# Sending the q and k norms and the softmax's inverse sums through DRAM in a two-layer hybrid block

## The chip, the cores and the metric

One core of a Trainium2 chip runs the whole program. Its engines are PE (TensorE, matrix products into PSUM), DVE (VectorE), ACT (ScalarE), POOL (GpSimd) and SP (SyncE, which here only issues transfers). Each executes its own list of instructions in order and waits on semaphores of the others. The metric is device microseconds of one execution, median of several runs; lower is better.

## The reference

Two layers over 256 latent tokens with a prefix of 256 context tokens, model width 1024. A layer normalizes and modulates its input, projects it, and feeds three branches: a state-space scan ("ssd"), attention, and a gated MLP. Their outputs are projected, gated and summed; then comes a SwiGLU. The part that matters here is attention:

```python
def rmsnorm(t, w):
    tf = t.astype(jnp.float32)
    tf = tf * lax.rsqrt(jnp.mean(tf * tf, axis=-1, keepdims=True) + EPS)
    return tf.astype(t.dtype) * w
...
    return rmsnorm(q, q_norm), rmsnorm(k, k_norm), v      # 8 heads of 64 features
...
    p = softmax(concatenate([s_lat, s_ctx]))               # latent queries: 512 keys, with a bias
    out = p @ [v_lat, v_ctx]
    s = q @ k.T * Dh ** -0.5; p = softmax(s); out = p @ v  # context queries: 256 keys (layer 0 only)
```

So every head's q and k (per token) is multiplied by one over the root of its mean square, and every row of the softmax by one over its sum.

## The kernel before

Activations lie feature by token: 128 features on the partitions, 512 tokens (256 context, 256 latent) along the free axis. Weights come from DRAM in 316 tiles of 128 x 1024 (`wr`, five buffers in the pool `raw`). ACT rounds each to float32r (`hi`, L222), DVE takes the rest (`lo`, L232), and three products of float32r parts stand for one product in float32 (`mm3`, L246). `ws.low` of a tile also has SP load the tile three further on. Tiles `T` (128 x 512) come from a ring of 61, `S` from eight PSUM banks; a tile that is asked for again makes its first writer wait for the last user of the old one.

The order of work is written out by hand. `gemm` (L275) issues the big products and calls `tick` after every fourth k-step. A tick stands for four k-steps of 512 columns (twelve products); it advances the clock, runs what `later` set down for that time, and takes steps of three queues of generators, "ssd", "att" and "mod", at rates of their own (att: 1.0 steps a tick at first, then `R_ATT`, 0.85 in layer 0 and 1.0 in layer 1). Each `yield` ends a step. So small work of the branches is threaded between big products, on all engines at once.

What the change touches:

- `qk_tile` leaves q and k and their squares in SBUF. `qk_norm` (L1066), once for k and once for q in each layer, sums the squares of each head by a small product into PSUM (two rows per group of 32 partitions hold the two heads of tile j), takes root and reciprocal of all 128 x 512 values, splits the result into two float32r parts placed on different partitions (`RQ`, L1086 and L1087), and after a few more steps has PE spread it for each j over 128 partitions (`pair_rows`, L1092); DVE multiplies q or k by that (L1094). In layer 1 q has 256 columns.
- `attention` takes head after head. An item is one head of the context or the latent queries: 16 items in layer 0 (ctx, ctx, lat, lat for each pair of heads), 8 in layer 1 (lat only). At step t it issues the output product of the pair that ended at t - 4 (`pv_out`), the transposes of item t - 2 (`transp`), and the scores of item t. Scores: PE, DVE adds the bias and takes the maximum (L1141, L1160), ACT takes the exponential with its row sum. Half a tick later `rest` takes one over the sum and multiplies the probabilities by it (L1148 to L1150, L1169 to L1172), before PE transposes them (L1186).
- `pv_out`: ACT rounds the result from PSUM (L1202), DVE takes the rest from PSUM (L1203).
- `bias_load`: SP refills a ring of four bias tiles at once when their next head is known.

Of the kernel before, what the change touches and what calls it, by code (L numbers as in the profile page):

```python
# [80 lines left out]
D_0 = (3, 6)  # L81
D_1 = (6, 3)
Q_0 = (1, 2)
Q_1 = (3, 5)
Q_2 = (6, 3)
L_G = (4, 4)
Z_S = (1.5, 3.0)
Y_S = (2.0, 0.5)
# [1 line left out]
G_S = (1.0, 0.5)  # L90
F_LAG = (3, 3)
FA = 2


@with_exitstack
def kernel(ctx: ExitStack, tc: tile.TileContext, a, out):
# [19 lines left out]
    def T(s="t", dt=F32):  # L116
        return tpool.tile([128, TOK], dt, tag="t", name=nm(s))
# [25 lines left out]
    for e, f in ((epsb, 1.0), (eps4, 4.0), (eps64, 64.0)):  # L143
        DVE.memset(e, f * EPS)
    mk = cpool.tile([128, 256], F32, name="mk")
    selp = cpool.tile([128, 8, 128], F32R, name="selp")
    lom = cpool.tile([128, 1], F32, name="lom")
    ident = cst[:, C_ID:C_ID + 128]
    ones = cst[:, C_ONE:C_ONE + 128]

# [454 lines left out]
    for l in range(NL):  # L605
# [5 lines left out]
        def pcol(c, n=1):  # L611
            return P[:, c:c + n]
# [32 lines left out]
        if not last:  # L645
            SP.dma_start(out=cst[:, 0:C_ONE], in_=a["cst"][:, 0:C_ONE])
            SP.dma_start(out=cst[:, C_COS:C_ROW], in_=a["cst"][:, C_COS:C_ROW])
            SP.dma_start(out=cst[:, C_BS:C_MF], in_=a["cst"][:, C_BS:C_MF])
            SP.dma_start(out=mk, in_=a["cst"][:, C_MF:NC_])
            DVE.tensor_copy(selp.rearrange("p a (b c) -> p a b c", c=64),  # L650
                            cst[:, C_SP:C_SP + 16].rearrange("p (a b) -> p a b", b=2).unsqueeze(3).to_broadcast(
                                [128, 8, 2, 64]))

            DVE.tensor_reduce(out=lom, in_=cst[:, C_ROW + 4:C_ROW + 8], op=ADD, axis=AX.X)
            DVE.tensor_scalar(lom, lom, -1.0, None, MUL)

        def token_major(n0, evac, between=()):

# [113 lines left out]

        Fd = dpool.tile([64, 2, 128], F32, name=nm("Fd"))
        Cd = dpool.tile([16, 4, 128], F32, name=nm("Cd"))

        def pair_rows(j, pr):

            return selp[:, 2 * j + pr]

        def dt_gen():  # L780
            for _ in range(D_0[l]):
# [284 lines left out]
        def qk_norm(kind):  # L1066

            b = 0 if kind == "k" else c0
            for _ in range(Q_0[l]):
                yield  # L1070
            ps = S()
            for j in range(4):
                mm(ps[32 * j:32 * j + 32, b:], cst[:, C_BS:C_BS + 32], qsq.pop((kind, j))[:, b:])
            rq, RQ = T("rq"), T("RQ", F32R)
            if kind == "q":
                ACT.activation(rq[:, b:], ps[:, b:], AF.Sqrt, bias=eps64)
            else:
                ACT.activation(rq[:, b:], ps[:, b:], AF.Sqrt, scale=1.0 / 64, bias=epsb)
            table(AF.Exp)
            for c in range(b, 512, 256):  # L1080
                DVE.reciprocal(rq[:, c:c + 256], rq[:, c:c + 256])
                yield
            for _ in range(Q_1[l]):
                yield

            ACT.copy(RQ[:, b:], rq[:, b:])  # L1086
            DVE.scalar_tensor_tensor(RQ[:, b:], RQ[:, b:].bitcast(F32), lom, rq[:, b:], MUL, ADD)  # L1087
            for _ in range(Q_2[l]):
                yield
            for j in range(4):  # L1090
                ps = S()
                mm(ps[:, b:], pair_rows(j, 0), RQ[:, b:])  # L1092
                t = qk[kind, j]
                DVE.scalar_tensor_tensor(t[:, b:], t[:, b:], pcol(P_KN if kind == "k" else P_QN),  # L1094
                                         ps[:, b:], MUL, MUL)
                yield

        def attention():
# [30 lines left out]
            def score(ps, hd, q0, n):  # L1129
                Q, lo, K = st[hd]  # L1130
                mm(ps, Q[:, q0:q0 + 128], K[:, 0:n], True, False)
                mm(ps, lo[:, q0:q0 + 128], K[:, 0:n], False, True)

            def scores_lat(hd):
                pr = []
                st_ = small(8, "ast")
                for qt in (0, 1):
                    bt = T("bt")
                    ps = S()
                    score(ps, hd, 256 + qt * 128, 512)  # L1140
                    DVE.tensor_tensor_reduce(out=bt, in0=ps, in1=biases[2 * hd + qt], op0=ADD, op1=MAX, scale=1.0,  # L1141
                                             scalar=-3.0e38, accum_out=st_[:, qt:qt + 1])
                    DVE.tensor_scalar(st_[:, 2 + qt:3 + qt], st_[:, qt:qt + 1], -1.0, None, MUL)
                    ACT.activation(bt, bt, AF.Exp, bias=st_[:, 2 + qt:3 + qt], accum_out=st_[:, 4 + qt:5 + qt])
                    pr.append(bt)

                def rest():
                    DVE.reciprocal(st_[:, 6:8], st_[:, 4:6])  # L1148
                    for qt in (0, 1):
                        DVE.tensor_scalar(pr[qt], pr[qt], st_[:, 6 + qt:7 + qt], None, MUL)  # L1150

                later(A_N[l], rest)
                return pr

            def scores_ctx(hd):
                st_ = small(8, "ast")
                ps = S()
                for qt in (0, 1):
                    score(ps[:, qt * 256:qt * 256 + 256], hd, qt * 128, 256)
                DVE.tensor_reduce(out=st_[:, 0:2], in_=ps.rearrange("p (q k) -> p q k", q=2), op=MAX, axis=AX.X)  # L1160
                DVE.tensor_scalar(st_[:, 2:4], st_[:, 0:2], -1.0, None, MUL)
                p = T("pc")
                for qt in (0, 1):
                    sl = slice(qt * 256, qt * 256 + 256)
                    ACT.activation(p[:, sl], ps[:, sl], AF.Exp, bias=st_[:, 2 + qt:3 + qt],
                                   accum_out=st_[:, 4 + qt:5 + qt])

                def rest():
                    DVE.reciprocal(st_[:, 6:8], st_[:, 4:6])  # L1169
                    for qt in (0, 1):  # L1170
                        sl = slice(qt * 256, qt * 256 + 256)
                        DVE.tensor_scalar(p[:, sl], p[:, sl], st_[:, 6 + qt:7 + qt], None, MUL)  # L1172

                later(A_N[l], rest)
                return p

            def transp(s_, pr):
# [14 lines left out]
            def pv_out(s_, j, pts):  # L1192
                ps = S()
                nk = 4 if s_ else 2
                for kt in range(nk):
                    for q in (0, 1):
                        hd = 2 * j + q
                        mm(ps[64 * q:64 * q + 64, 0:256], va[kt][:, hd * 64:hd * 64 + 64],
                           pts[q][kt // 2][:, (kt % 2) * 256:(kt % 2) * 256 + 256], kt == 0, kt == nk - 1)
                hi, lo, b = yna[j]  # L1200
                sl = slice(s_ * 256 - b, s_ * 256 + 256 - b)
                ACT.copy(hi[:, sl], ps[:, 0:256])  # L1202
                DVE.tensor_tensor(lo[:, sl], ps[:, 0:256], hi[:, sl], SUB)  # L1203

            items = [(j, s_, q) for j in range(4) for s_ in ((1,) if last else (0, 1)) for q in (0, 1)]
            pr, pts = {}, {}
# [5 lines left out]
            for t in range(len(items) + A_P[l]):  # L1212
# [13 lines left out]
                if t < len(items):  # L1226
                    j, s_, q = items[t]
                    pr[t] = (scores_lat if s_ else scores_ctx)(2 * j + q)
                    if s_ and 2 * j + q < 6:
                        bias_load(2 * j + q + 2)  # L1230
                if heads and (last or t % 2):
                    stack(heads.pop(0))
                yield
# [455 lines left out]
```

## Time and profile before

| | us |
|---|---|
| median of 3 runs (1603.38 to 1606.58) | 1603.64 |
| profiled execution, its own time | 1604.21 |
| its span in the profile | 1602.4 |
| PE, DVE, ACT busy in the span | 1578.7, 1163.1, 830.5 |

The profiled execution's time is 1.8 us longer than its span. PE's granted clock is 0.997 of full speed over the span. "Busy" of PE counts the modelled length of overlapping products: back-to-back products overlap, so the distance from one start to the next says what a product costs, not its length. Layer 0's qk_norms lie at about 140 to 260 us and its attention at about 350 to 460; layer 1's at about 1100 to 1210 and 1235 to 1317.

### The profile page before, as it was taken

To read this page: it belongs to the slowest core of one execution; us is meant where nothing else is said; L and a number is where in the kernel's file an instruction comes from. 1 tells how busy PE (TensorE), PEld (TensorE's weight loads), DVE (VectorE), ACT (ScalarE), POOL (GpSimd) and SP (SyncE) were. 2 spreads that over 40 slices of the span, in tenths; PEclk is the share of its full clock that TensorE was granted. 3 is DMA by queue.
4 is the path that set the end of the run, shared out by engine and by line. 5 is a ranking of instruction groups with operands and counts; after the bars stand their busy time and mean duration, and the time that the engine had idled before them with its cause. 6 is when DMAs were issued, how large, how long until landed. Compare 5 with 4: busy or idle time off the path is not lost.

```text
span 1602.4 us, 23608 instructions
## 1 busy us (share of the span) xinstructions
PE 1578.7 (99%) x8908; PEld 1325.2 (83%) x8909; DVE 1163.1 (73%) x2005; ACT 830.5 (52%) x1551; POOL 6.9 (0%) x21
## 2 busy tenths in 40 slices
PE   8999999999999999999999999999999999999999
PEld 5878787777678888988888888978888989998888
DVE  5467889777868766676666654778988987687764
ACT  4456876656643233433223212667676785466652
POOL 0000000000000000000000000000000000000000
PEclk9999999999999999999999999999999999999999
DMA  9513433443344545354556775525434456656654
GB/s 331 206 53 115 125 105 107 122 141 92 107 135 142 183 148 193 122 177 155 180 172 198 260 241 185 174 92 161 130 115 138 134 157 183 199 167 192 194 178 138
DMA packets 87345, 254.37 MB, mean 159 GB/s; under 512 B 10560, under 2 KB 19008, under 8 KB 87104
## 3 DMA queue, kind: packets, MB, share of 16 engines
q1 hardware_dynamic: 87232, 252.87, 49.3%
q8 instruction: 70, 1.15, 0.3%
q14 instruction: 43, 0.35, 0.1%
HBM read 248.44 MB, written 4.39 MB: 158 GB/s over the span
## 4 chain that ended last, share of the span: by engine, by line
PE 79%; DVE 11%; ACT 5%; DMA 3%; issue 2%; SPq 0%; ACTq 0%; DVEq 0%
PE g L126 71%; PE s L126 6%; DVE lo L232 3%; DVE xbc L718 2%; DMA wm<-in_wmod 2%; ACT hi L222 1%; PE s L1186 1%; ACT M L987 1%; DVE scr L192 1%; DVE bt L1141 1%; DVE M L896 0%; DMA x<-in_xT 0%; ACT rb L987 0%; DVE ks L1114 0%; PE rs L126 0%
## 5 line engine op out<-in xcount | busy, mean ns | idle before, releaser
L126 PE MATMUL g<-hh,hi 128*128 128x512 f32 (+1 forms) x1280 | 471.4, 368 | 0.1
L126 PE MATMUL g<-hh,lo 128*128 128x512 f32 (+1 forms) x1280 | 462.1, 361 | 1.4 <-DVE lo L232 1.4
L126 PE MATMUL g<-hl,hi 128*128 128x512 f32 (+1 forms) x1280 | 462.1, 361 | 0.5 <-DVE hl L551 0.4
L232 DVE TENSOR_TENSOR lo<-wr,hi 128x1024 fp32r<-128x1024 f32 x316 | 382.5, 1219 | 78.1 <-ACT hi L222 77.6
L222 ACT CAST hi<-wr 128x1024 fp32r<-128x1024 f32 x316 | 323.8, 1046 | 37.7 <-DMA wr<-in_ws 31.8
L126 PEld LDWEIGHTS g<-hh,hi 128*128 128x128 f32 x1280 | 241.8, 189 | 49.0 <-issue 11.5
L126 PEld LDWEIGHTS g<-hh,lo 128*128 128x128 f32 x1280 | 241.6, 189 | 40.8 <-DVE lo L232 3.4
L126 PEld LDWEIGHTS g<-hl,hi 128*128 128x128 f32 x1280 | 242.0, 189 | 37.1 <-DVE hl L551 1.1
L192 DVE SCALAR_TENSOR_TENSOR scr<-wm,csil 128x1024 bf16<-128x1024 f32 x128 | 156.1, 1220 | 63.4 <-DMA wm<-in_wmod 63.3
L126 PE MATMUL g<-hp,hi 128*128 128x512 f32 x304 | 105.7, 391 | 0.0
L718 DVE SCALAR_TENSOR_TENSOR xbc<-g,pv,xbc 128x508 f32<-128x508 f32 (+3 forms) x128 | 91.3, 713 | 9.5 <-ACT xbc L712 6.4
L126 PE MATMUL g<-hp,lo 128*128 128x256 f32 x304 | 85.3, 281 | 0.9 <-DVE lo L232 0.8
L1295 ACT ACTIVATE th<-g,pv 128x512 f32<-128x512 f32 (+1 forms) x48 | 27.9, 580 | 95.9 <-PE g L126 91.6
L367 ACT CAST fh<-f 128x512 fp32r<-128x512 f32 x22 | 13.6, 620 | 112.9 <-DVE f L1447 112.9
L126 PE MATMUL g<-fh,lo 128*128 128x512 f32 x176 | 68.6, 390 | 0.4 <-DVE lo L232 0.4
L126 PE MATMUL g<-fh,hi 128*128 128x512 f32 x176 | 68.5, 389 | 0.0
L126 PE MATMUL g<-fl,hi 128*128 128x512 f32 x176 | 68.5, 389 | 0.0
L126 PEld LDWEIGHTS g<-hp,hi 128*128 128x128 f32 x304 | 56.9, 187 | 12.4
L126 PE MATMUL g<-lo,hh 128*128 128x256 f32 x224 | 63.7, 284 | 3.2 <-DVE lo L232 3.1
L126 PE MATMUL g<-hi,hh 128*128 128x256 f32 x224 | 64.6, 288 | 0.0
L126 PE MATMUL g<-hi,hl 128*128 128x256 f32 x224 | 63.3, 283 | 0.0
L126 PE MATMUL g<-fp,hi 128*128 128x512 f32 (+1 forms) x198 | 61.4, 367 | 0.0
(310 smaller groups left out, 2657.9 us busy)
## 6 DMA issues: line engine op xcount, KB each, us to landing
wr<-in_ws SPq DMA_DIRECT2D x316, 512.0 KB, 4.2
wm<-in_wmod SPq DMA_DIRECT2D x80, 512.0 KB, 4.4
rb<-Fd SPq DMA_DIRECT2D x48, 256.0 KB, 3.9
wm<-in_wm SPq DMA_DIRECT2D x32, 256.0 KB, 6.0
ex<-Cd SPq DMA_DIRECT2D x32, 128.0 KB, 3.6
bias<-in_rpb SPq DMA_DIRECT2D x32, 128.0 KB, 2.1
x<-in_xT SPq DMA_DIRECT2D x8, 256.0 KB, 6.1
xm<-in_xT SPq DMA_DIRECT2D x8, 256.0 KB, 5.3
```

The source lines that it names most:

```text
L126: PE.matmul(o, l, r, start=start, stop=stop)
L192: DVE.scalar_tensor_tensor(scr, raws[n], 1.0, csil[:, v, :], MUL, MUL, accum_out=modr[l][:, ft, v:v + 1])
L222: ACT.copy(hi, self.raw[i])
L232: DVE.tensor_tensor(lo, self.raw.pop(i), hi, SUB)
L367: ACT.copy(hi, src[:, c0:])
L718: DVE.scalar_tensor_tensor(av3[:, :, o0:o1], pv3[:, :, o0 + d:o1 + d], w(j), av3[:, :, o0:o1], MUL, ADD)
L987: ACT.activation(z, z, AF.Exp, bias=bias(st, d))
L1141: DVE.tensor_tensor_reduce(out=bt, in0=ps, in1=biases[2 * hd + qt], op0=ADD, op1=MAX, scale=1.0, scalar=-3.0e38, accum_out=st_[:, qt:qt + 1])
L1186: PE.transpose(ps[:, kt * 256 + qt * 128:kt * 256 + qt * 128 + 128], src, ident)
L1295: ACT.activation(th[:, c0:], ps[:, c0:], AF.Tanh, scale=0.5, bias=pcol(P_BG + br * 8 + m))
```

## The change

The spread over partitions by PE and the scaling of the probabilities by DVE are both replaced by transfers through DRAM. The diff, cut to its core:

```diff
-Q_1 = (3, 5)
-Q_2 = (6, 3)
+B_L = (1.0, 0.5)
+I_A = (1.0, 0.75)
+I_B = (1.0, 1.0)
...
-    selp = cpool.tile([128, 8, 128], F32R, name="selp")
-    lom = cpool.tile([128, 1], F32, name="lom")
...
 qk_norm:
-            rq, RQ = T("rq"), T("RQ", F32R)
+            n = 512 - b
+            t, w = T("rq"), small(32, "rqs", 2)
+            Nd, Ni = (dpool.tile([8, n], F32, name=nm("Nd")) for _ in range(2))
+            ACT.copy(t[:, b:], ps[:, b:])
+            yield
+            yield
+            for j in range(4):
+                SP.dma_start(out=Nd[2 * j:2 * j + 2], in_=t[32 * j:32 * j + 2, b:])
+            flat = lambda z: z.rearrange("h t -> (h t)").rearrange("(p c) -> p c", p=128)
+            w = w[:, 0:n // 16]
+            for _ in range(2):
+                yield
+            SP.dma_start(out=w, in_=flat(Nd))
+            for _ in range(2):
+                yield
             if kind == "q":
-                ACT.activation(rq[:, b:], ps[:, b:], AF.Sqrt, bias=eps64)
+                ACT.activation(w, w, AF.Sqrt, bias=eps64)
...
             table(AF.Exp)
-            for c in range(b, 512, 256):
-                DVE.reciprocal(rq[:, c:c + 256], rq[:, c:c + 256])
-                yield
-            for _ in range(Q_1[l]):
-                yield
-            ACT.copy(RQ[:, b:], rq[:, b:])
-            DVE.scalar_tensor_tensor(RQ[:, b:], RQ[:, b:].bitcast(F32), lom, rq[:, b:], MUL, ADD)
-            for _ in range(Q_2[l]):
-                yield
+            DVE.reciprocal(w, w)
+            yield
+            yield
+            SP.dma_start(out=flat(Ni), in_=w)
+            R = {}
+            def spread(j):
+                R[j] = T("RQ")
+                for a_ in (0, 1):
+                    SP.dma_start(out=R[j][64 * a_:64 * a_ + 64, b:],
+                                 in_=Ni[2 * j + a_].unsqueeze(0).to_broadcast([64, n]))
+            yield
+            yield
+            spread(0)
+            yield
+            yield
             for j in range(4):
-                ps = S()
-                mm(ps[:, b:], pair_rows(j, 0), RQ[:, b:])
                 t = qk[kind, j]
+                if j < 3:
+                    spread(j + 1)
                 DVE.scalar_tensor_tensor(t[:, b:], t[:, b:], pcol(P_KN if kind == "k" else P_QN),
-                                         ps[:, b:], MUL, MUL)
+                                         R.pop(j)[:, b:], MUL, MUL)
                 yield
 attention:
+            Pd = dpool.tile([16, 256], F32, name=nm("Pd"))
+            inv = {}
+            def inverse(s_, hd, st_):
+                DVE.reciprocal(st_[:, 6:8], st_[:, 4:6])
+                j, q = divmod(hd, 2)
+                if q == 0:
+                    inv[s_, j] = small(256, "inv", 3)
+                row, y = Pd[s_ * 8 + hd], inv[s_, j]
+                def back():
+                    SP.dma_start(out=y[64 * q:64 * q + 64, :], in_=row.unsqueeze(0).to_broadcast([64, 256]))
+                def away():
+                    SP.dma_start(out=row.rearrange("(q p) -> p q", p=128), in_=st_[:, 6:8])
+                    later(I_B[l], back)
+                later(I_A[l], away)
...
-                    DVE.reciprocal(st_[:, 6:8], st_[:, 4:6])
-                    for qt in (0, 1):
-                        DVE.tensor_scalar(pr[qt], pr[qt], st_[:, 6 + qt:7 + qt], None, MUL)
-                later(A_N[l], rest)
+                later(A_N[l], lambda: inverse(1, hd, st_))
...                                    (the same for the context items)
 pv_out:
-                ACT.copy(hi[:, sl], ps[:, 0:256])
-                DVE.tensor_tensor(lo[:, sl], ps[:, 0:256], hi[:, sl], SUB)
+                y = inv.pop((s_, j))
+                DVE.tensor_tensor(y, y, ps[:, 0:256], MUL)
+                ACT.copy(hi[:, sl], y)
+                DVE.tensor_tensor(lo[:, sl], y, hi[:, sl], SUB)
...
-                        bias_load(2 * j + q + 2)
+                        later(B_L[l], lambda n=2 * j + q + 2: bias_load(n))
```

DVE in layer 0's attention, around the output of the first pair of heads, before (`pc` the context probabilities, `ast` the sums and their inverses, `ynl` the low part of the output):

```order
L1169 RECIPROCAL ast_3594<-ast_3594 128x2
L1172 TENSOR_SCALAR pc_3602<-pc_3602,ast_3594 128x256 x2
L1203 TENSOR_TENSOR ynl_3624<-s_3625,ynh_3623 128x256
L1160 TENSOR_REDUCE ast_3646<-s_3647 128x2
L1161 TENSOR_SCALAR ast_3646<-ast_3646 128x2
```

and in the changed kernel (`inv` the inverse sums as they came back):

```order
L1150 RECIPROCAL ast_3609<-ast_3609 128x2
L1223 TENSOR_TENSOR inv_3438<-inv_3438,s_3641 128x256
L1225 TENSOR_TENSOR ynl_3640<-inv_3438,ynh_3639 128x256
L1186 TENSOR_REDUCE ast_3663<-s_3664 128x2
L1187 TENSOR_SCALAR ast_3663<-ast_3663 128x2
```

The two scalings of the probabilities are gone, and a product of the output with the inverse sums stands ahead of its low part, which ACT's rounding now separates from it.

DVE in layer 0's q norm, before (`rb` and `M` belong to the scan, `lo` is a weight's low part; the reciprocals of 128 x 256 stand twice, some 25 rows earlier):

```order
L994 TENSOR_TENSOR rb_2075<-rb_2075,cb_2038 128x512
L896 TENSOR_TENSOR M_2193<-rb_2164,mk 128x512
L232 TENSOR_TENSOR lo_2176<-wr_1935,hi_2175 128x1024
L741 TENSOR_TENSOR xbc_2083<-xbc_2083,cst 128x256
L1005 SCALAR_TENSOR_TENSOR xbc_1647<-xbc_1647,pv_176,s_2224 128x256
```

and in the changed kernel:

```order
L983 TENSOR_TENSOR rb_2083<-rb_2083,cb_2042 128x512
L885 TENSOR_TENSOR M_2200<-rb_2171,mk 128x512
L1084 RECIPROCAL rqs_1963<-rqs_1963 128x32
L231 TENSOR_TENSOR lo_2183<-wr_1930,hi_2182 128x1024
L734 TENSOR_TENSOR xbc_2091<-xbc_2091,cst 128x256
```

The reciprocal, now of 128 x 32, stands right ahead of a weight's low part, and behind ACT's root of the same step.

SP at the start of layer 0's attention, before (`wr` weights, `bias` the bias tiles):

```order
L212 DMA wr_3378<-in_ws 128x1024
L212 DMA wr_3428<-in_ws 128x1024
L1127 DMA bias_3329<-in_rpb 128x256
L1127 DMA bias_3330<-in_rpb 128x256
L212 DMA wr_3511<-in_ws 128x1024
```

and in the changed kernel (`Pd` a row of inverse sums in DRAM):

```order
L211 DMA wr_3394<-in_ws 128x1024
L211 DMA wr_3443<-in_ws 128x1024
L1160 DMA Pd_3352<-ast_3408 128x2x1
L1157 DMA inv_3438<-Pd_3352 64x256
L211 DMA wr_3524<-in_ws 128x1024
L1160 DMA Pd_3352<-ast_3455 128x2x1
L1138 DMA bias_3344<-in_rpb 128x256
L1138 DMA bias_3345<-in_rpb 128x256
```

Each item's row goes out and comes back between the weights' loads, and the bias tiles are asked for later.

## Rows read from the trace of the kernel before

**Rows 1.** The page's busy times: engine, us, share of the span, instructions.
```profile
PE 1578.7 (99%) x8908; PEld 1325.2 (83%) x8909; DVE 1163.1 (73%) x2005; ACT 830.5 (52%) x1551; POOL 6.9 (0%) x21
```

**Rows 2.** What PE waited for: engine, line, releaser: us in total, times, longest.
```profile
PE g L126 <- DVE lo L232: 5.7, 8, 2.2
PE s L1186 <- DVE pc L1172: 3.5, 2, 2.1
```

**Rows 3.** Busy time by stretch: us, PE, PEld, DVE, ACT, POOL, PEclk, DMA share, GB/s.
```profile
130.00:260.00 130.00, 125.56 (x654) 98.80 (x653) 113.67 (x186) 92.79 (x202) 0.00 (x0) 1.00 0.40 119
340.00:470.00 130.00, 125.48 (x645) 98.08 (x645) 104.83 (x222) 80.09 (x166) 4.26 (x9) 0.99 0.36 114
```

**Rows 4.** PE in order of time, layer 0's k norm: start, us, instruction, count.
```profile
177.93 0.58 PE L126 MATMUL s<-RQ,selp 128*128 128x512 f32 x1
178.35 0.40 PE L126 MATMUL g<-hh,hi 128*128 128x512 f32 x1
178.58 0.40 PE L126 MATMUL g<-hl,hi 128*128 128x512 f32 x1
...
182.22 0.50 PE L126 MATMUL s<-RQ,selp 128*128 128x512 f32 x1
182.56 0.40 PE L126 MATMUL g<-hh,hi 128*128 128x512 f32 x1
```

**Rows 5.** PE in order of time, layer 1's q norm.
```profile
1201.08 0.28 PE L126 MATMUL s<-RQ,selp 128*128 128x256 f32 x1
1201.19 0.40 PE L126 MATMUL g<-hh,hi 128*128 128x512 f32 x1
...
1204.63 0.47 PE L126 MATMUL s<-RQ,selp 128*128 128x256 f32 x1
1204.94 0.40 PE L126 MATMUL g<-hh,hi 128*128 128x512 f32 x1
```

**Rows 6.** The tile RQ on PE: count, ns min/median/max, first and last start, shapes.
```profile
L126 PE MATMUL s<-RQ,selp x16: 278/486/580, 177.9 to 1207.7; 128*128 128x512 f32 x12, 128*128 128x256 f32 x4
```

**Rows 7.** PE's gaps in layer 0, in brackets the idle time ahead and its releaser.
```profile
199.98 0.39 PE L126 MATMUL g<-lo,hh 128*128 128x256 f32 x1 [0.93 <-DVE lo L232]
...
246.31 0.39 PE L126 MATMUL g<-lo,hh 128*128 128x256 f32 x1 [2.18 <-DVE lo L232]
...
254.63 0.47 PE L126 MATMUL s<-RQ,selp 128*128 128x512 f32 x1 [1.34 <-DVE xbc L718]
...
407.18 0.71 PE L1186 MATMUL s<-cst,pc 128*128 128x128 f32 x4 [1.45 <-DVE pc L1172]
...
431.90 0.90 PE L1186 MATMUL s<-cst,pc 128*128 128x128 f32 x4 [2.05 <-DVE pc L1172]
```

**Rows 8.** ACT in order of time: the last of the exponential behind the second gap.
```profile
429.45 0.20 ACT L1165 ACTIVATION_READ_ACCUMULATOR pc<-s,ast 128x1 f32 x1
```

**Rows 9.** Lines that the change removes or resembles: count, ns min/median/max, first and last start.
```profile
L1150 DVE TENSOR_SCALAR bt<-bt,ast x32: 479/485/490, 370.9 to 1305.2; 128x512 f32<-128x512 f32 x32
L1172 DVE TENSOR_SCALAR pc<-pc,ast x16: 333/352/702, 358.1 to 436.7; 128x256 f32<-128x256 f32 x16
L1081 DVE RECIPROCAL rq<-rq x7: 1740/1746/1753, 141.9 to 1166.5; 128x256 f32<-128x256 f32 x7
L1203 DVE TENSOR_TENSOR ynl<-s,ynh x8: 411/416/425, 379.9 to 460.3; 128x256 fp32r<-128x256 f32 x8
```

**Rows 10.** ACT's table load at the q norm's root.
```profile
L1076 ACT ACT_TABLE_LOAD  x2: 1283/1283/1283, 193.8 to 1164.7; - x2
```

**Rows 11.** Transfers: instruction, count, KB each, median us from issue to landing.
```profile
wr<-in_ws SPq DMA_DIRECT2D x316, 512.0 KB, 4.2
...
ex<-Cd SPq DMA_DIRECT2D x32, 128.0 KB, 3.6
...
Cd<-R SPq DMA_DIRECT2D x8, 8.0 KB, 1.4
```

**Rows 12.** What SP waited for between 135 and 265 us: total, times, longest.
```profile
SPq L888 <- PE s L126: 18.0, 6, 5.7
```

More of the change, by code (lines that the diff above doesn't have):

```diff
@@ L649 @@
             SP.dma_start(out=mk, in_=a["cst"][:, C_MF:NC_])
[L650 to L655, printed above, removed]
         def token_major(n0, evac, between=()):
@@ L774 @@
         Cd = dpool.tile([16, 4, 128], F32, name=nm("Cd"))
-        def pair_rows(j, pr):
-            return selp[:, 2 * j + pr]
         def dt_gen():
@@ L1075, in qk_norm @@
+            w = w[:, 0:n // 16]
[4 more added lines that the diff above has]
+                yield
             if kind == "q":
-                ACT.activation(rq[:, b:], ps[:, b:], AF.Sqrt, bias=eps64)
+                ACT.activation(w, w, AF.Sqrt, bias=eps64)
             else:
-                ACT.activation(rq[:, b:], ps[:, b:], AF.Sqrt, scale=1.0 / 64, bias=epsb)
+                ACT.activation(w, w, AF.Sqrt, scale=1.0 / 64, bias=epsb)
@@ L1145, in scores_lat @@
                     pr.append(bt)
-                def rest():
-                    DVE.reciprocal(st_[:, 6:8], st_[:, 4:6])
-                    for qt in (0, 1):
-                        DVE.tensor_scalar(pr[qt], pr[qt], st_[:, 6 + qt:7 + qt], None, MUL)
-                later(A_N[l], rest)
+                later(A_N[l], lambda: inverse(1, hd, st_))
                 return pr
@@ L1166, in scores_ctx @@
                                    accum_out=st_[:, 4 + qt:5 + qt])
[L1168 to L1174, printed above, removed]
+                later(A_N[l], lambda: inverse(0, hd, st_))
                 return p
```

## Prediction

> **What bounds the kernel now.** I read the page's busy times first: PE is busy 1578.7 of 1602.4 us, DVE 73% and ACT 52% [rows 1]. All of PE's idle time is the rest, 1602.4 − 1578.7 = 23.7 us, part of it at the very start where nothing can be computed yet. So a change can gain in two ways only: fewer products on PE, or less of that idle time. The second view, what PE waited for, names what matters of the idle time here: a weight's low part from DVE (5.7 us in 8 waits, the longest 2.2) and the scaled context probabilities, also from DVE (3.5 us in 2 waits, nearly all of it) [rows 2]. Third, the busy time by stretch shows where DVE is close to the bound: 113.67 of 130 us in 130 to 260 (the q and k norms of layer 0) and 104.83 of 130 in 340 to 470 (its attention), with PE's clock at 1.00 and 0.99 and the DMA engines at 0.40 and 0.36 [rows 3]. I take no gain from gaps of layer 1.
>
> The profiled execution took 1604.21 us, 0.57 above the median 1603.64. The sum below is made against 1604.21, and 0.57 is taken off at the end.
>
> **Term 1: sixteen products leave PE.** The tile RQ is read by 16 products, 12 of 512 columns and 4 of 256 [rows 6]. Their listed length (486 ns median) overlaps that of the next, so the price of one is a distance between starts. Wide ones, in layer 0's k norm: 177.93 to 178.35 = 0.42, and 182.22 to 182.56 = 0.34; an ordinary product beside it takes 178.35 to 178.58 = 0.23 [rows 4]. Narrow ones, layer 1's q norm: 1201.08 to 1201.19 = 0.11, and 1204.63 to 1204.94 = 0.31 [rows 5]. The lower bound takes the ordinary distance: 12 x 0.23 + 4 x 0.11 = 3.2 us. The upper one: 12 x 0.42 + 4 x 0.31 = 6.3. I take the mean of the two readings for each kind, 12 x 0.38 = 4.6 and 4 x 0.21 = 0.8, together **−5.4 us**: both wide readings lie well above the ordinary distance. These products stand between big ones on an engine that never rests, so nothing hides their going.
>
> [...]
>
> **Term 2: the transposes no longer wait for DVE.** In layer 0's attention PE stands still for 1.45 us ahead of the transposes at 407.18 and for 2.05 us ahead of those at 431.90, both times for the scaled probabilities [rows 7]. ACT had written the last of the exponential's sum at 429.65 (429.45 + 0.20), 2.25 us ahead of the transposes' start [rows 8], and PE had begun to wait at 429.85. The changed transposes read the unscaled probabilities, which are complete then. So the whole gap goes, if nothing else is late there. What could be next is a weight's low part. But DVE loses 32 scalings at 0.485 and 16 at 0.352, 21.1 us, and gets 12 products of 128 x 256 at 0.416, 5.0 us [rows 9]; two thirds of both are layer 0's (16 and 16 scalings, 8 products: −13.4 + 3.3 = −10.1 us), in a stretch where DVE is busy for 104.8 of 130 us [rows 3]. I take 3.3 of the 3.5 us: **−3.3 us** (bounds 0 and −3.5).
>
> **Term 3: the q and k norms' relief of DVE.** Here three gaps stand in layer 0: 0.93 and 2.18 for a low part, 1.34 for a DVE result of the scan's branch, 4.45 us in all [rows 7]. DVE loses 7 reciprocals of 1.746 us [rows 9], four of them in this stretch (7.0 us), and two low halves of RQ over 512 columns, by twice the 0.352 of a 256-column scaling (estimate) 0.7 each, 1.4; it gets two reciprocals of 32 columns, a sixteenth of 3.5 us, 0.2 each. So about 8.0 us less in 113.7. A gap goes only if the removed work stood in the queue close ahead of it; a 1.7 us reciprocal can lie anywhere in 30 us. I take half: **−2.2 us** (bounds 0 and −4.45).
>
> **Term 4: new waits.** Each can only lengthen.
> - DVE's small reciprocal stands right ahead of a low part in three of the four norms, and behind ACT's root of the same step. ACT has to load a table before the q root, 1.283 us [rows 10], and works through its own queue first. While DVE waits there, a low part is late, and PE may wait for it. Before, the reciprocal of 128 x 256 waited for the same root at the same kind of place, and the gaps above contain that. Bounds 0 and 3 x 1.28 = 3.8 us.
> - In the output of a pair, ACT now rounds what DVE made, and DVE's low part waits for ACT: one step to DVE more. Queued behind it is the maximum of the next item's scores, then ACT's exponential. Cost at most ACT's backlog, 12 times; what covers it is that the transposes come two steps after the scores. I put it at nothing, upper bound 12 x 0.42 (the length of the new product) = 5.0.
> - The root's input goes out and back, and the inverses go out and are spread: small writes of 8 KB landed in 1.4 us before, 128 KB spreads in 3.6, weights in 4.2 [rows 11]. The code gives each of these about two steps. In attention a step is (431.90 − 407.18) / 4 = 6.2 us [rows 7], since the two places are one round of four items apart; at 0.85 steps a tick, a tick is 5.3 us. The row of sums has one tick to land (5.3 against 1.4 us), the row read back about 4.7 − 2.5 = 2.2 ticks (11.7 us against 3.6): half a tick to the reciprocal and one to each transfer go off the four steps to the output. Hidden. The new bytes, 16 spreads of two transfers of 128 KB (half of that for layer 1's q) and 24 of 64 KB, are under 6 MB beside 316 weights of 512 KB, with the DMA engines 60% idle in these stretches [rows 3].
> I take **+1.0 us** for the whole term, near its lower bound, since the nearest rows leave every transfer time to spare.
>
> The other edits go at nothing, each beside busy DVE or ACT time that PE does not wait for. ACT copies 512 columns in place of rounding them, and its roots shrink from 512 to 32 columns; DVE's scaling of q and k reads RQ from SBUF rather than PSUM (bounds: 0.1 us either way, sixteen times, 1.6); the set-up of the spreading matrix leaves the start, where PE waits for data (0 to −0.5). The bias tiles, asked for up to a tick later, were asked for two heads ahead, over 12 us, and land like any transfer of 128 KB in 3.6 us at most.
>
> Sum: −5.4 − 3.3 − 2.2 + 1.0 = −9.9, 1604.2 − 9.9 = 1594.3; less 0.57 gives 1593.7, **1594 us**.
>
> **Rivals.**
> - *More relief.* All gaps above go, 3.5 + 4.45, and the rest of the low parts' waits with them, 5.7 − 0.93 − 2.18 = 2.6 [rows 2, 7]; the products give 6.3 and nothing new waits: 1604.2 − 16.9 − 0.6 = 1587. For it: DVE is the releaser everywhere. Against it: gaps that a handshake with ACT makes stay. Chance 0.12.
> - *Only the products.* The two long gaps of attention and those of the norms return under another name (a low part, y for ACT): 1604.2 − 5.4 − 0.6 = 1598, with the lower price of the products 1600.4. For it: in a program ordered by hand, each wait taken away has let the next one come up. Chance 0.14, half of it within 0.2%.
> - *The gains cancel.* New waits at their upper bounds, 3.8 + 5.0, against the sum's 10.9 without them: 1603.6 − 10.9 + 8.8 = 1601.5, and up to 1603.6 with the lower price of the products. Chance 0.07.
> - *SP in order (slower).* SP issues every transfer in turn, and a spread whose tile T is still in use holds all behind it. In 135 to 265 us SP already waited six times for such a tile, 18.0 us in all, the longest 5.7 [rows 12], and the change takes more tiles from the same ring there. If each of the eight spreads of layer 0 is held for 5.7 us and lands 3.6 later, 9.3 us, against a norm's step of (182.22 − 177.93) = 4.3 [rows 4], DVE stands 5.0 us for each, 40 us. DVE has 130 − 113.7 = 16.3 us idle there, and 8.0 of relief; 15.7 would reach PE: 1604.2 − 5.4 − 3.3 + 15.7 − 0.6 = 1610.6. It begins to cost beyond a hold of 0.7 us per spread on DVE, on PE beyond 3.0 more. Against it: SP's waits were harmless before, since it runs far ahead of the engines, and the spread is asked for a step ahead. Chance 0.05.
> - *The inverse sums come late (slower).* A row of sums leaves as 256 separate numbers from 128 partitions. If that takes long, the output's product with the inverses is late, DVE stands with low parts behind it, and PE with it. It decides only when the write takes over 5.3 us (SP's read back then waits for it, and the weights behind it) or the read over 11.7, against 1.4 and 3.6 in the rows [rows 11]; each microsecond over that comes 12 times, so 2 over would give 1594 + 24 = 1618. Chance 0.04. [...]
>
> **How the numbers follow.** What is left for the forecast is 0.58, with 1590 to 1599 as its own range: all of term 3 and the upper price of the products give 1590, the lower price with none of term 3 1598.5. A measurement of this kernel can tell about 0.2% (3.2 us) from no change: faster means below 1600.4. Faster: 0.58 + 0.12 + 0.07 = 0.77. Within: 0.07 + 0.07 = 0.14. Slower: 0.05 + 0.04 = 0.09. From 1587 to 1603 the range holds the forecast, half or more of the relief, all of the products alone and half of the cancelling, 0.8 or a little over.
>
> **What the changed profile would show.** Term 1: PE's busy time lower by about 5 us, 16 products fewer, and no tile RQ on PE. Term 2: no gap ahead of the transposes at about 400 and 425 us, and DVE some 10 us less busy in its attention. Term 3: DVE 8 us less busy in 130 to 260, and about two of the three gaps there gone or shorter. Term 4: PE waits for a low part right behind a reciprocal of 128 x 32 in small pieces at most; DVE's waits for `inv`, `RQ` and the rounded output near nothing. SP's rival would show as spreads whose releaser is PE or DVE and DVE's scaling of q and k idle ahead for microseconds; the other as a landing of the sums above 5 us. The forecast is wrong if PE's idle time does not fall, or if one of DVE's new waits, on a transfer or on ACT, costs PE more than 3 us.

## The result and the profile after

The changed kernel takes 1639.35 us (median of 4 runs, 1638.71 to 1641.56) against 1603.88 us before: ratio 1.0219, interval 1.0204 to 1.0234. It is 2.2% slower, 45 us from the forecast and 36 us above the upper end of its range.

The page's busy times, after (as [rows 1]):

```profile
PE 1589.5 (97%) x8893; PEld 1330.4 (81%) x8893; DVE 1136.4 (69%) x1959; ACT 831.3 (51%) x1551; POOL 6.9 (0%) x21
```

DVE is relieved, by 27 us over the span. But the span grew from 1602.4 to 1637.3, and PE stands still for 1637.3 − 1589.5 = 47.8 us of it instead of 23.7. PE's busy time rose too, although it has 16 products fewer. What PE waited for, after (as [rows 2]):

```profile
PE g L127 <- DVE lo L231: 18.6, 11, 4.7
PE s L127 <- DVE inv L1223: 6.7, 2, 6.5
PE g L127 <- ACT ynp L1224: 4.4, 1, 4.4
...
PE s L127 <- ACT pt L1208: 3.8, 2, 2.5
```

The waits for the scaled probabilities are gone, as forecast. In their place stand waits for low parts, three times as much as before, and for the product with the returned sums. Their places, PE's larger gaps after (as [rows 7]):

```profile
202.31 0.58 PE L127 MATMUL g<-lo,hh 128*128 128x256 f32 x1 [3.86 <-DVE lo L231]
254.05 0.58 PE L127 MATMUL g<-lo,hh 128*128 128x256 f32 x1 [4.66 <-DVE lo L231]
433.86 0.58 PE L127 MATMUL s<-ks,qs 128*128 128x256 f32 x1 [6.49 <-DVE inv L1223]
473.18 3.31 PE L127 MATMUL s<-pt,va 128*64 128x256 f32 x14 [2.46 <-ACT pt L1208]
1348.23 1.04 PE L127 MATMUL g<-ynp,hi 128*128 128x256 f32 x2 [4.42 <-ACT ynp L1224]
```

Layer 0's norms and both layers' attentions have them. Why busy time rose is in the busy times by stretch, after (columns as [rows 3]; the first two answer to it):

```profile
130.00:260.00 130.00, 120.96 (x597) 94.12 (x596) 96.96 (x166) 88.96 (x195) 0.00 (x0) 0.95 0.43 128
340.00:470.00 130.00, 121.72 (x620) 94.99 (x618) 89.62 (x187) 74.79 (x160) 4.25 (x9) 0.97 0.50 109
200.00:210.00 10.00, 7.69 (x43) 5.81 (x44) 8.11 (x10) 1.22 (x2) 0.00 (x0) 0.66 0.23 57
430.00:440.00 10.00, 6.14 (x18) 4.81 (x20) 5.99 (x14) 5.21 (x11) 0.00 (x0) 0.66 0.53 111
```

Behind the large gaps the granted clock is 0.66 over ten microseconds. What running products lost by it is PE's busy time times one minus the granted clock; summed over slices of 1 us, that comes to 15.6 us after and 5.0 before. So the budget, an estimate, is: 24.1 us more idle time, 10.6 us more at the low clock, 2.8 us in the last 150 us (left open below) and about 3.2 us of products less (below), 34.3 of the 34.9 us by which the span grew.

By place: the same instruction (ACT's tanh in the MLP) starts 7.6 us later than before at 297 us, behind layer 0's norms; 19.1 at 485, behind its attention; 20.3 at 1241; and 32.1 at 1322, behind layer 1's attention. The two attentions cost 11.5 and 11.8 us, the norms some 9, nearly all of it in layer 0.

SP shows the attention's cause. What it waited for at the read back, over the whole span:

```profile
SPq L1157 <- DMA Pd<-ast: 110.6, 21, 8.7
```

and SP in order of time in layer 0's attention:

```profile
412.06 0.42 SPq L1160 DMA_DIRECT2D Pd<-ast  x1
412.54 1.39 SPq L1138 DMA_DIRECT2D bias<-in_rpb  x2
414.03 0.38 SPq L1160 DMA_DIRECT2D Pd<-ast  x1
421.85 0.45 SPq L1157 DMA_DIRECT2D inv<-Pd  x1
422.41 0.52 SPq L211 DMA_DIRECT2D wr<-in_ws  x1
423.35 0.38 SPq L1160 DMA_DIRECT2D Pd<-ast  x1
423.84 0.45 SPq L1157 DMA_DIRECT2D inv<-Pd  x1
```

The row written at 412.06 can be read back at 421.85 only, 9.4 us after its issue ended, and SP issues nothing from 414.4 to 421.85, the weight behind it included. The write was taken to land in 1.4 us; it takes 9.4. By the trace's completion events, counted from the end of the issue, the 24 writes of the sums land after 7.1 to 14.1 us, 9.8 at the median. What is read back late is then waited for by DVE, and DVE by PE (the 6.49 us at 433.86):

```profile
DVE inv L1223 <- DMA inv<-Pd: 31.0, 6, 8.2
```

The norms show another cause. ACT in order of time in layer 0's k norm, after:

```profile
161.43 0.69 ACT L976 ACTIVATE rb<-rb,nB 128x128 f32<-128x128 f32 x2 [1.04 <-DVE M L885]
162.03 1.27 ACT L976 ACTIVATE M<-M,nB 128x128 f32<-128x128 f32 x4
163.31 1.28 ACT L1082 ACT_TABLE_LOAD   x1
164.60 0.32 ACT L1082 ACTIVATE rqs<-rqs,eps 128x32 f32<-128x32 f32 x1
164.94 1.28 ACT L376 ACT_TABLE_LOAD   x1
166.24 0.20 ACT L376 ACTIVATE dummy<-eps 128x1 f32<-128x1 f32 x1
166.35 0.56 ACT L1047 COPY q<-g 128x512 f32<-128x512 f32 x1
```

The small root takes 0.32 us, its table loads there and back and the dummy, an operation that only brings the exponential's table back, 2.8. Before, the root stood where ACT waited for PE in any case:

```profile
139.01 1.28 ACT L1078 ACT_TABLE_LOAD   x1
141.17 0.69 ACT L1078 ACTIVATE rq<-s,eps 128x512 f32<-128x512 f32 x1 [0.88 <-PE s L126]
```

Now it stands where ACT has no idle time behind it until 177.5 us, and holds q's copy (166.35 us, before 164.07), a weight's rounding and a scan result back by 2.3 us each.

### The profile page after: what moved, and what is told of

The parts are those of the page before. It is cut to its first block, busy times and chain, and to the rows that moved or that the text cites. A ratio compares the mean times of both kernels' runs of the same rounds, so it can differ in the third digit from the quotient of the medians.

```text
span 1637.3 us, 23745 instructions
## 1 busy us (share of the span) xinstructions
PE 1589.5 (97%) x8893; PEld 1330.4 (81%) x8893; DVE 1136.4 (69%) x1959; ACT 831.3 (51%) x1551; POOL 6.9 (0%) x21
## 4 chain that ended last, share of the span: by engine, by line
PE 59%; DMA 6%; DVE 3%; ACT 3%; issue 1%; SPq 0%; DVEq 0%; ACTq 0%
PE g L127 56%; DMA Pd<-ast 3%; PE s L127 2%; DMA wm<-in_wmod 2%; DVE lo L231 1%; ACT hi L221 1%; DMA inv<-Pd 1%; DVE xbc L711 0%; DMA rb<-Fd 0%; PE s L1206 0%; DVE scr L191 0%; ACT M L976 0%; DVE hx L435 0%; DVE xm L1411 0%; PE rs L127 0%
## 5 line engine op out<-in xcount | busy, mean ns | idle before, releaser
L221 ACT CAST hi<-wr 128x1024 fp32r<-128x1024 f32 x316 | 323.9, 1046 | 37.8 <-DMA wr<-in_ws 35.9
L127 PEld LDWEIGHTS g<-hh,lo 128*128 128x128 f32 x1280 | 243.1, 190 | 47.7 <-DVE lo L231 10.2
L127 PEld LDWEIGHTS g<-hp,hi 128*128 128x128 f32 x304 | 57.1, 188 | 14.1
```

Source lines behind the costliest of these rows:

```text
L127: PE.matmul(o, l, r, start=start, stop=stop)
L221: ACT.copy(hi, self.raw[i])
```

## The experiments

Each was compared with the kernel before on the same chip (medians 1603.7 to 1604.9). The first four part the change.

**Norms alone.** The attention is that of before.

> The changed q and k norms with the attention of before (its scalings of the probabilities and its bias loads). In the changed kernel PE runs 7.6 us late by the end of layer 0's norms and another 1.3 us by the end of layer 1's; the rest of the 35 us (11.5 and 11.8) comes up inside the two attentions. Theory 1 (the two parts cost separately, attention most): 1603.9 + 8.9 = about 1613 us. Rival 2 (SP, held in order by the norms' transfers, loses its lead, and attention only shows it): 1625 us or more. Rival 3 (the norms' part alone is the gain that was forecast, and only attention's transfers spoil it): 1597 us or less.

Measured: 1613.34 us, 1.0051 (1.0034 to 1.0068). This is theory 1: there are two separate costs, and the norms' part is a loss by itself.

**Sums written, but not awaited; and not written.**

```diff
-in_=row.unsqueeze(0).to_broadcast([64, 256])
+in_=a["cst"][s_ * 8 + hd, 0:256].unsqueeze(0).to_broadcast([64, 256])
 # second kernel, besides:
-SP.dma_start(out=row.rearrange("(q p) -> p q", p=128), in_=st_[:, 6:8])
```

> The changed kernel, but the inverse sums are read back from a constant table in DRAM rather than from the row just written (so the output is not scaled by the sums); the writes of 256 four-byte pieces still go out at the same places and nobody waits for them. Theory 1a (the landing of that write, about 9.7 us against the tick of 5.3, is awaited by SP's read back and all behind it): the attentions' 23.3 us go, 1639.4 - 23 = 1616, and with the forecast relief of attention 1613. Rival 1b (the small pieces keep the DMA engines busy and slow the weights down): 1630 us or more.

> As the last one (constant inverse sums read back), and the writes of the sums are left out altogether. Theory 1a: within 2 us of the last one, 1613 to 1616. Rival 1b (load on the DMA engines): about 1613, with the last one at 1630 or more. Rival 1c (the cost is in the extra hop from DVE to ACT and back in the output of a pair, or in the read back, not in the write): both stay above 1630.

Measured: 1625.63 us (1.0136, 1.0115 to 1.0157) and 1602.86 (0.9994, 0.9983 to 1.0005). Both theories hold a part: of 36.5 us, waiting for the landing is 13.7, and the mere presence of the writes 22.8. A write can also hold SP until the sums are there, but that is not where the 22.8 us lie: SP waits 29.9 us for it here and 37.8 us in the run with larger pieces below, which loses far less. The extra hop (1c) costs nothing that shows. Busy times of layer 0's attention, with the unawaited write and without it:

```profile
340.00:470.00 130.00, 124.96 (x642) 96.62 (x638) 92.39 (x193) 77.98 (x166) 4.25 (x9) 0.97 0.72 113
```

```profile
340.00:470.00 130.00, 129.05 (x674) 100.96 (x673) 101.66 (x207) 82.12 (x172) 4.25 (x9) 1.00 0.44 133
```

With 16 writes of 1 KB the DMA engines are busy 0.72 of the time rather than 0.44, and move less, 113 GB/s against 133. It is not the small pieces that fill them. By the packets' records of these two traces, all packets of four bytes take 9 ns at the median and 0.03 of the engines' time; the rest of the increase stands on the packets of other transfers. Those of 4 KB, mostly weights, take up to 7.5 us each instead of 1.8, and 0.47 of the engines' time instead of 0.32, although they are fewer.

**Fewer pieces; larger pieces.**

```diff
-SP.dma_start(out=row.rearrange("(q p) -> p q", p=128), in_=st_[:, 6:8])
+SP.dma_start(out=row[0:128].unsqueeze(1), in_=st_[:, 6:7])                       # half the pieces
+SP.dma_start(out=row.rearrange("(p c) -> p c", p=128), in_=st_[:, 6:38])         # pieces of 128 B
```

> The changed kernel with only the first 128 of each row's 256 sums written (128 pieces of four bytes) and read back twice; half of the inverse sums are wrong. If the landing goes by the number of pieces, it takes about 5 us instead of 9.7, within the tick of 5.3, SP's wait for it falls from 110 us to under 20, and the time is near that of the kernel whose write nobody awaits, 1613 to 1618. If it is a fixed latency of such a write, nothing changes: 1637 to 1640.

> The changed kernel, where the write of a row of sums consists of 128 pieces of 128 bytes (32 copies) rather than 256 of four bytes; the read back takes 256 of these numbers, so the inverse sums are wrong. With 128 pieces of four bytes the landing was still 7 to 10 us. Theory 3a (the size of a piece, four bytes, makes it slow): landing 3 to 5 us as that of the norms' inverses with pieces of the same size, SP's wait under 20 us, 1603 to 1612. Rival 3b (any write of so many pieces from 128 partitions behind the weights takes that long): 1640 to 1650.

Measured: 1648.70 us (1.0276, 1.0231 to 1.0320) with half the pieces, SP's wait 121.0 us in 19 times. The writes land after 7.3 to 16.2 us, 10.2 at the median: the landing does not go by the number of pieces. With 128 pieces of 128 bytes, 16 times the data of the changed kernel's write: 1609.39 (1.0032, 1.0019 to 1.0044). The writes land after 1.1 to 3.9 us, 2.3 at the median, behind the same weights, and SP waits 5.6 us in 4 times for them. The size of the pieces is what makes the landing late (3a), and 30 of the 36.5 us go with it. Why half the pieces are 9 us slower than all of them is not settled; their rows are also read back in pieces of half the size.

**Written at once.** `I_A = (0.0, 0.0)`, `I_B = (2.0, 1.75)`.

> The changed kernel, its sums written without delay after the reciprocal and read back at the same time as before, so that the write has two ticks (10.6 us) to land instead of one. Theory 1a (part of the loss is SP waiting for the landing): SP's wait at the read back falls from 110 to under 30 us, and what is left is the load of the small pieces, near the kernel whose write nobody awaits, 1624 to 1628. Rival (SP is now held for the reciprocal instead): 1637 or more.

Measured: 1661.20 us (1.0355, 1.0320 to 1.0390). The rival holds. SP now waits 65.9 us for the reciprocal and still 47.4 for landings:

```profile
SPq L1160 <- DVE ast L1150: 65.9, 17, 10.7
...
SPq L1157 <- DMA Pd<-ast: 47.4, 9, 9.2
```

The delay that the change puts ahead of the write is worth 22 us against this.

**The norms' four repairs.** The first three are single steps on the norms alone: the reciprocal two steps behind the root; every transfer a step sooner; the k norm a step shorter, so that q's head sums stand where they stood.

> The kernel with the changed norms alone, its small reciprocal moved two steps behind the root (the transfers after it one step later). There DVE waits 2.96 and 3.12 us for ACT's root in layer 0, and PE later stands 3.88 and 4.66 us for a low part. Theory 2a (DVE is the bound from there to the low part, and starts that much late): the two gaps shrink by about 3 us each and most of the lower clock behind them goes, 1613.3 - 6 to 9 = 1604 to 1607 us. Rival 2b (the gaps come from the scalings of k and q, which now stand right ahead of the low parts, and from PE arriving earlier): 1611 to 1614.

> The kernel with the changed norms alone, with its transfers asked for one step after their data's operation in place of two (the reciprocal one step behind the root); the scalings of k and q come three steps sooner. Rival 2b: they leave the queue ahead of the late low part, and the gap there shrinks, 1603 to 1608. Theory 2a alone: as in the first of these runs by the reciprocal, 1604 to 1609. If SP, issuing sooner than the data, is held and the weights suffer: 1614 or more.

> The kernel with the changed norms alone, the k norms one step shorter (one step fewer between the first spread and the first scaling). The q norm follows in the same queue and starts one step late in the changed kernel: its head sums stand behind products that wait for a low part, so ACT, which copies them, waits 7.4 us for PE, and DVE 6.4 us behind it. One step less puts the head sums of layer 0's q back where they stood before. Theory 2c (the whole norm part's loss comes from that step): 1613.3 down to 1602 to 1606. Rival 2b (the stretch is bound by DVE whatever the step, scalings right ahead of the low parts): 1610 or more.

> The same with the small reciprocal two steps behind the root (its later start of the q norm taken back too). If DVE's 3 us waits for ACT's root cost as well, it is 2 to 4 us below the last one; if ACT is late there anyway and the wait only moves to the next low part, within 1.5 us of it.

Measured: 1611.81, 1614.72, 1610.77 and, with the first and the third together, 1611.59 us, against 1613.34. Theories 2a and 2c fall: neither the wait at the reciprocal nor the late step is worth over 2.6 us, and asking for the transfers sooner gains nothing. In the first, DVE's wait for the root is gone and one of 3.3 us for a weight's rounding by ACT stands in its place: ACT was late, not the reciprocal early. Rival 2b, that DVE is the bound there whatever ACT does, is left by these four and decided by the next run.

**The root before the trip.**

```diff
-            ACT.copy(t[:, b:], ps[:, b:])
+            ACT.activation(t[:, b:], ps[:, b:], AF.Sqrt, ...)
+            table(AF.Exp)
 ...
-            ACT.activation(w, w, AF.Sqrt, ...)
-            table(AF.Exp)
             DVE.reciprocal(w, w)
```

> The kernel with the changed norms alone, the root taken of all 512 columns where the sums leave PSUM (in place of ACT's copy, where ACT has waited 2 us for PE, and where the kernel before takes it), so that only the small reciprocal is left after the trip. In the changed norms the two table loads, the root and a dummy take ACT 162.3 to 165.4, in a stretch where ACT stands still nowhere from 160.5 to 172, and everything behind comes late: ACT's copy of q, the weight's rounding, DVE's low parts. Theory 2d (that is the norms' loss): the gaps of 3.9 and 4.7 us come down towards 0.9 and 2.2 and the lower clock behind them goes: 1613.3 to 1600 to 1605. Rival 2b (DVE is the bound there whatever ACT does): 1610 or more.

> The same with the k norm one step shorter, so that layer 0's q norm starts at the step at which it started before. That step alone gave 2.5 us (1613.3 to 1610.8). If the two causes add, 2 to 3 us below the last one; if the late step only mattered through ACT's lateness, no difference.

Measured: 1602.34 us (0.9988, 0.9977 to 0.9998) and 1602.33 (0.9990, 0.9981 to 1.0000). Theory 2d holds and 2b falls: moving the root back is worth 10 to 11 us (by the ratios and by the medians), and with it the late step costs nothing. ACT in order of time, and PE's gaps, in the first of the two:

```profile
138.18 1.28 ACT L1070 ACT_TABLE_LOAD   x1
140.36 0.69 ACT L1070 ACTIVATE rq<-s,eps 128x512 f32<-128x512 f32 x1 [0.90 <-PE s L127]
141.06 1.28 ACT L376 ACT_TABLE_LOAD   x1
```

```profile
198.49 0.39 PE L127 MATMUL g<-lo,hh 128*128 128x256 f32 x1 [2.40 <-DVE lo L231]
...
244.84 0.38 PE L127 MATMUL g<-lo,hh 128*128 128x256 f32 x1 [1.50 <-DVE lo L231]
```

Here one table load hides in ACT's wait for PE. These gaps are back to 3.9 us, from 8.5, and in the profiled execution the granted clock is 1.0 over the span.

**Scaling by PE.** POOL makes diagonal matrices of the inverse sums, and PE multiplies by them instead of transposing; on the norms with the k norm a step shorter, and on the kernel before.

> The norms of the first of these runs, and an attention without transfers: the idle POOL makes a diagonal matrix of each 128 inverse sums, and PE multiplies the probabilities by it in place of transposing them, so that they are scaled on the way and DVE scales nothing. With the sums in time and no write, the attention of the changed kernel was 10.5 us faster than that of before (1602.9 against 1613.3). If that comes from DVE's relief, this attention gains 6 to 10 us as well: 1594 to 1600 with the first run at 1604. If POOL is late, or the products cost PE more than transposes, 1604 or more.

> The kernel before with that attention alone (its q and k norms as they were; half of the spreading matrix, which nothing read, is left out for room). By DVE's relief in the attention: 1603.7 - 6 to 10 = 1594 to 1598. If products with the diagonal cost PE over 0.05 us more than a transpose, 160 of them, 1602 or more.

Measured: 1619.34 us (1.0098, 1.0083 to 1.0113) and 1614.95 (1.0068, 1.0051 to 1.0085). A miss. The waits for scaled probabilities went, but each product with a diagonal stands twice in the trace, 256 entries for 128 products, where each transpose of `pc` before stands once (32 entries for 32):

```profile
L126 PE MATMUL s<-dg,bt x256: 270/275/377, 373.1 to 1315.8; 128*128 128x128 f32 x128
```

PE's busy time on the kernel before rises from 1578.7 to 1595.2, more than all that could be won.

**Large pieces, complete.** With the root before the trip, PE turns a pair's inverse sums (128 x 2 to 2 x 128) in the unused half of the output's PSUM tile, ACT copies them out, and the pair leaves in four pieces of 512 bytes; each layer's first pair leaves as in the change.

```diff
+            for q in (0, 1):
+                PE.transpose(ps[0:2, 256 + 128 * q:384 + 128 * q], sts[q][:, 6:8], ident)
+            ACT.copy(y[0:2], ps[0:2, 256:512])
 ...
+            SP.dma_start(out=Pd[...].rearrange("h (q p) -> q h p", p=128),
+                         in_=y[0:2].rearrange("q (h p) -> q h p", p=128))
```

> The changed kernel, complete, with two mends: the root as in the first of these runs, and the inverse sums of a pair of heads turned by PE (128 x 2 to 2 x 128, in the half of the output's PSUM tile that nothing uses, one pair ahead) so that they leave in four pieces of 512 bytes; only the first pair of each layer still leaves in pieces of four bytes. Theory 1 + 3a (small pieces load the DMA engines and land late; in time, the attention's relief is worth 10 us): with the first run at 1602, 1592 to 1597. If turning (24 small products, a rounding on ACT) costs what it gives, 1600 to 1604; if a row back to partitions is late whatever the pieces, 1610 or more.

Measured: 1599.82 us, 0.9981 (0.9969 to 0.9992): 0.2% faster than the kernel before and 2.4% than the changed one, but not the 1592 to 1597 expected. What PE waited for, and SP in order of time:

```profile
PE g L129 <- DVE lo L233: 6.6, 8, 2.4
PE s L129 <- ACT state L955: 2.7, 4, 0.7
```

```profile
415.66 0.26 SPq L1181 DMA_DIRECT2D Pd<-inv  x1
417.81 1.18 SPq L1139 DMA_DIRECT2D bias<-in_rpb  x2
419.10 1.09 SPq L1177 DMA_DIRECT2D inv<-Pd  x2
```

A row is read back 3.4 us after its write, and no wait for probabilities is left. SP's waits for rows of 512 bytes are 9.6 us in 5 times over the span; another 26.0 us in 4 times are for the first pairs' rows, still in pieces of four bytes. The expected 10 us came from the difference of two kernels, the norms alone and the one without the writes. In their profiled executions the granted clock over the span was 0.993 in the first and 0.996 in the second, so part of the difference was clock, an estimated 5 us (0.007 of 1611.5 us against 0.004 of 1602.3). With the root mended the granted clock is 1.0 over the span of both profiled executions (the root's repair alone and this run), and no low clock is left to win: the attention's gaps were 3.5 us, PE's idle time fell from 24.0 to 21.0 us, and the medians differ by 2.5 us, with ranges that overlap (1599.5 to 1605.9 and 1599.0 to 1605.4).

## Why the prediction was wrong

The step that failed is in term 4, "small writes of 8 KB landed in 1.4 us before", taken for a row of inverse sums. The row has 1 KB in 256 pieces; its landing is 9.8 us at the median. With it failed "Hidden": a tick of 5.3 us does not cover it. The rival for this was written down with the right wait ("SP's read back then waits for it, and the weights behind it") and a chance of 0.04. By its price, 12 us for each microsecond over 5.3, a landing of 9.4 gives 1594 + 49 = 1643. That this is near 1639 is luck: the wait is only 13.7 us of the loss.

The larger part failed in the sentence behind "Hidden", which set the new bytes, "under 6 MB", against DMA engines "60% idle in these stretches" and put their load at nothing. In bytes that is right. But the writes' presence costs 22.8 us in the run where nobody waits for them, and there packets of 4 KB, mostly of the weights, take up to 7.5 us instead of 1.8. No rival of the prediction had this.

The nearest row by size was not the nearest by shape: the time falls from 1639.4 with pieces of four bytes to 1609.4 with 128, where nothing written gives 1602.9.

Term 4 also mis-sized the root. It counted one table load of 1.283 us a root, as DVE's wait, and 3.8 us at most. The root with both loads is 3.1 us on ACT, at a place without slack, and moving it back alone won 10 to 11 us, the low clock behind the gaps included. The diff moves the root past six steps; ACT's idle time at the old place, and its lack at the new one, stood in the trace of before.

Term 1 was mis-sized. The products did go, but by the distances between starts their price is their lower bound, 3.2 us; no run measures them alone. PE in order of time at the place of [rows 4], after:

```profile
177.73 1.02 PE L127 MATMUL s<-xbc,state 128*128 128x256 f32 x4
178.40 0.58 PE L127 MATMUL g<-hh,hi 128*128 128x512 f32 x1
178.82 0.40 PE L127 MATMUL g<-hl,hi 128*128 128x512 f32 x1
179.05 0.40 PE L127 MATMUL g<-hh,lo 128*128 128x512 f32 x1
```

An ordinary product in the removed one's place, behind the scan's four products, has the same 0.42 us to the next. So here the long distance came with the place and not with the removed product, and a product taken out saves the ordinary 0.23 (an estimate from these distances), not the 0.38 that was taken.

Term 2's mechanism was right: the waits for probabilities went in every variant with scaling behind the product, and with the sums in time DVE's extra hop cost nothing. Its size came out as some 2.5 us of 3.3 (large pieces against the root's repair alone, with the cost of turning the sums in it), which lies within the scatter of the runs.

Term 3 failed as an average. Its relief was right: with the root mended, PE does the work of before in 130 to 260 us (650 products against 654), and DVE is busy for 105.56 us instead of 113.67, 8.1 less. (In the changed kernel it is 16.7 less, but part of that is work that comes later, with 597 products.) The relief did not stand where the gaps end. The k norm's reciprocals stood from 141.9 us on [rows 9], where DVE had waits to spare, while the low part at 200 us ends a stretch from 170 on in which DVE is busy for 29.45 of 30 us before and 29.48 with the root mended. Relief ahead of an idle time fills nothing but the idle time. With the root mended, the two gaps for low parts were 3.9 us, against 3.1 before; the third, 1.34, was gone, and one of 0.8 for the scan had come: 4.7 us instead of 4.45, where about half was forecast to go.

The rival on SP held for tiles was not it: SP did wait for a spread's tile (9.0 us once in layer 0's norms), but it does so with the root mended too. That SP is held in order did decide the attention, but for a landing.

One sum of the prediction is off without a consequence: "the lower price with none of term 3" gives 1598.1 by its own terms, not 1598.5.

What stays open: why writes of four-byte pieces land late (9.8 us at the median) and packets beside them are slow (up to 7.5 us), why half the pieces were slower still, and the 2.8 us that the changed kernel lost over its last 150 us, where PE waits 0.8 us, as before, and the granted clock is 1.00. The last is not the change's: the profiled executions with the norms alone and with the root mended show some 3 us there as well, those with pieces of 128 bytes and with the root mended and the k norm shorter next to none.

## What to carry to other kernels

Price a transfer by the row that is nearest in shape, pieces and partitions, not in bytes; if there is none, measure it first, since everything that one in-order queue issues behind its landing waits with it (here SP issued nothing from 414.4 to 421.85 us), and small pieces can slow the transfers beside them (here packets of 4 KB took up to 7.5 us instead of 1.8). When an operation is moved, look at what its engine does at the new place, with all that it brings along: a root of 0.3 us can carry 2.8 us of table loads into a stretch that has no slack. Relief counts only in the stretch that ends in the wait (with the root mended, 8.1 us less of DVE in 130 to 260 us left the gaps at 4.7 us, against 4.45), and a gap saved is worth the low clock behind it as well, where there is one (2.3 to 3.0 us behind each of four gaps of the changed kernel).

## What the runs showed of the hardware

- Writes of 256 four-byte pieces landed 7.1 to 14.1 us after their issue in the changed kernel (median of 24: 9.8), writes of 128 such pieces after 7.3 to 16.2 (10.2), writes of 128 pieces of 128 bytes after 1.1 to 3.9 (2.3).
- The packets of four bytes took 9 ns each at the median, yet with 16 such writes in 130 us that nobody awaited the DMA engines' busy share was 0.72 instead of 0.44; packets of 4 KB took up to 7.5 us instead of 1.8, and 0.47 of the engines' time instead of 0.32. In the changed kernel, which awaits the same writes, the share was 0.50.
- After PE gaps of 3.9 to 6.5 us products of the changed kernel ran at a granted clock of 0.50 for a while (6.8 us that begin inside the gap, so 0.66 over 10 us; distances of 0.21 us for products of 256 columns, 0.12 at a granted 1.00): 2.3 to 3.0 us lost on top of each gap, counted from the first product behind it. A gap's price is not fixed. Behind the same two gaps of the norms (3.85 and 4.66 us) the run with half the pieces was granted 0.83 over 10 us, and behind the attention's second gap the clock fell before (2.05 us; granted 0.75 over 430 to 435) but not with the root mended (2.06 us).
